# A gated product (GLU): groups of four rows in three 64 KiB slots in place of two-row tiles with slots of their own for the output

## The chip, the cores and the metric

The kernel runs on one core of a Trainium2 chip. The metric is the device time of one execution in microseconds (us). The three runs of the kernel before took 933.14, 933.66 and 934.35 us; their median is 933.66 us. A profile of one more execution says where the time goes.

## What is computed

```python
def setup_inputs():
    return {
        "x": np.random.randn(8192, 8192).astype(np.float32),
    }

def reference(x: np.ndarray) -> np.ndarray:
    a, b = np.split(x, 2, axis=-1)
    return a * (1 / (1 + np.exp(-b)))
```

Each row of x has 8192 numbers; the left 4096 are multiplied by the sigmoid of the right 4096. 268.4 MB are read and 134.2 MB are written, in fp32. Nothing is used twice.

## The kernel before

Everything is in `_tiles`. A tile is 256 rows: two consecutive rows on each of the 128 partitions (R = 2, line 27), so one load brings 64 KiB to each partition, 8 MiB in all, and one store takes 32 KiB from each, 4 MiB in all. There are 32 tiles. On chip there are two input slots `x_sb` of 64 KiB per partition and two output slots `o_sb` of 32 KiB per partition (lines 34 and 35), 192 KiB together; tile i uses slots i % 2.

Per tile there are four kinds of work:

- the load (line 53), a DMA issued by SyncE (SP). It waits until the product of tile i - 2 has read the slot;
- the sigmoid (line 71) on ScalarE (ACT), in place on the right half of each row;
- the product (line 72) on VectorE (DVE), out of the input slot into the output slot;
- the store (line 65), a DMA issued by ACT, after the product.

Inner tiles do both rows at once, one instruction of 8192 elements per partition on each engine. The first and the last tile are cut into four parts of 2048 elements, and in the last tile each part is stored by itself (lines 60 to 63 and 84 to 86). One small copy of 16 x 512 bytes from x to out (line 41) goes through ACT's DMA queue ahead of all else; its bytes are overwritten later.

The order on each engine is the order of the code. `implied` (line 37) drops waits that follow from others; lines 75 to 79 put the wait for a free output slot on the sigmoid in odd tiles. SP's DMAs form one queue and ACT's another; both run on the same 16 DMA engines. A DMA of 128 partitions is 128 packets, eight on each engine, and one more packet per engine that raises the semaphore. `_launch_early` moves the first load to the start of the program and `_close_on_sync` shortens its end; neither is touched.

Of the kernel before, what the change touches and what calls it, by code (L numbers as in the profile page):

```python
# [8 lines left out]
def _tiles(ctx, tc, x, out):  # L9

    nc = tc.nc
    P = nc.NUM_PARTITIONS  # L20
    DEP = mybir.DependencyInfo(mybir.DependencyClass.Sync, mybir.DependencyReason.DATA)
    fp32 = mybir.dt.float32
    SIG = mybir.ActivationFunctionType.Sigmoid

    n_rows, n_cols = x.shape
    half = n_cols // 2
    R = 2
    SLOTS = 2
    n_tiles = n_rows // (P * R)
    x_t = x.rearrange("(n p r) m -> n p (r m)", p=P, r=R)  # L30
    out_t = out.rearrange("(n p r) m -> n p (r m)", p=P, r=R)

    pool = ctx.enter_context(tc.tile_pool(name="io", bufs=1))
    xs = [pool.tile([P, R * n_cols], fp32, name=f"x_sb{k}") for k in range(SLOTS)]
    os = [pool.tile([P, R * half], fp32, name=f"o_sb{k}") for k in range(SLOTS)]

    def implied(later, *earlier):
        for e in earlier:
            tc.declare_no_dep(later.ins, e.ins, reason="follows from the waits that are kept")

    warm = nc.scalar.dma_start(out=out[0:16, 0:P], in_=x[0:16, 0:P])
    tc.keep_in_program_order(warm)

    gone = [{k: [] for k in ("loads", "sigs", "muls", "stores")} for _ in range(SLOTS)]
    last_stores = [[] for _ in range(SLOTS)]
    for i in range(n_tiles):
        old = gone[i % SLOTS]
        freed = last_stores[i % SLOTS]
        now = {k: [] for k in old}
        rows = xs[i % SLOTS].rearrange("p (r h m) -> p r h m", r=R, h=2)  # L50
        packed = os[i % SLOTS].rearrange("p (r m) -> p r m", r=R)

        load = nc.sync.dma_start(out=xs[i % SLOTS], in_=x_t[i])
        implied(load, *old["loads"], *old["sigs"])
        now["loads"].append(load)

        if 0 < i < n_tiles - 1:
            parts = [(slice(0, R), slice(0, half))]
        else:
            w = half // 2  # L60
            parts = [
                (slice(r, r + 1), slice(c * w, (c + 1) * w)) for r in range(R) for c in range(2)
            ]
        def store(cols):
            ins = nc.scalar.dma_start(out=out_t[i, :, cols], in_=os[i % SLOTS][:, cols])  # L65
            now["stores"].append(ins)

        chunks = []
        for k, (r, c) in enumerate(parts):
            b = rows[:, r, 1, c]  # L70
            sig = nc.scalar.activation(out=b, in_=b, func=SIG)  # L71
            mul = nc.vector.tensor_mul(out=packed[:, r, c], in0=rows[:, r, 0, c], in1=b)  # L72
            implied(sig, *old["sigs"], *old["muls"], *old["loads"])
            implied(mul, *old["muls"], *old["loads"], *now["loads"])
            by_sigmoid = i % 2 == 1 and len(parts) == 1
            implied(mul, *(s for s in old["stores"] if by_sigmoid or s not in freed))
            if by_sigmoid:
                for s in freed:
                    tc.add_manual_dep(sig.ins, s.ins.name, DEP, reason="frees the output slot")
            tc.keep_in_program_order(sig)  # L80
            now["sigs"].append(sig)
            now["muls"].append(mul)
            chunks.append(slice(r.start * half + c.start, r.start * half + c.stop))
            if i == n_tiles - 1 and k > 0:
                store(chunks[k - 1])
        store(chunks[-1] if i == n_tiles - 1 else slice(0, R * half))
        for s in now["stores"]:
            implied(s, *old["loads"], *old["sigs"], *old["muls"], *now["loads"], *now["sigs"])
        for k in old:
            old[k] += now[k]  # L90
        last_stores[i % SLOTS] = now["stores"]


def _launch_early(nc):
# [68 lines left out]
@with_exitstack  # L163
def kernel(
    ctx: ExitStack,
    tc: tile.TileContext,
    x: bass.AP,
    out: bass.AP,
):
    nc = tc.nc  # L170
    with ExitStack() as pools:
        _tiles(pools, tc, x, out)
    tc.close()
    tc.compile()
    _launch_early(nc)
    _close_on_sync(nc)
# [30 lines left out]
```

## Time and profile before

| what | value | from |
|---|---|---|
| median of three runs | 933.66 us | the times |
| span of the profiled execution | 932.3 us | the page |
| first load lands, first sigmoid | 21.91 us | the timeline |
| issue of a store | 0.36 us of ACT's queue | the timeline |
| issue of a load to its landing | 42.2 us, median | the page's DMA issues |
| issue of a 4 MiB store to its landing | 34.8 us, median | the page's DMA issues |
| last load lands, last sigmoids | 915.17 us | the timeline |

The span runs from the first to the last instruction that the profiler saw, so it is a little shorter than the time of an execution. A load's time to landing includes what lies ahead of it in its queue and what the other queue moves at the same time: it isn't the time of 8 MiB alone. The page counts DMA in two ways, as the share of time in which the 16 engines hold a packet, and as GB/s. The records put all bytes of a packet at its start, so the GB/s of a stretch mean something only where the stretch is long or begins and ends between the starts of packets.

### The profile page before, as it was taken

The numbers are of one execution on the slowest core, as the hardware profiler recorded it, in microseconds if no ns is written. First come the engines' busy times: TensorE is split into PE (matmuls) and PEld (weight loads), VectorE is DVE, ScalarE is ACT, GpSimd is POOL, SyncE is SP. The second block draws the span as 40 slices with busy tenths as digits, with TensorE's granted clock in tenths as the row PEclk, the third lists the DMA queues.
The fourth block names the chain that finished last, engine by engine and source line by source line (L and its number), as shares of the span: only waits on it lengthen the run. The fifth ranks groups of instructions, "written<-read, shape, count | busy, mean of one in ns | idle before, by whom it ended". The sixth has DMA issues, their size and how long they took to land.

```text
span 932.3 us, 250 instructions
## 1 busy us (share of the span) xinstructions
DVE 278.6 (30%) x38; ACT 227.0 (24%) x39; POOL 0.2 (0%) x4
## 2 busy tenths in 40 slices
DVE  0333213333133331233312333123331233312333
ACT  1323330233311333113331133311333203332033
POOL 0000000000000000000000000000000000000000
DMA  9999999999999999999999999999999999999999
GB/s 405 427 450 427 418 457 408 450 427 427 450 418 437 427 427 450 427 427 453 444 408 430 441 456 428 416 458 408 450 427 427 450 416 439 427 433 444 426 429 405
DMA packets 9681, 402.67 MB, mean 432 GB/s; under 512 B 1088, under 2 KB 1104, under 8 KB 1104
## 3 DMA queue, kind: packets, MB, share of 16 engines
q1 hardware_dynamic: 4608, 268.44, 66.6%
q10 hardware_dynamic: 5072, 134.23, 33.4%
q14 instruction: 1, 0.01, 0.0%
HBM read 268.44 MB, written 134.23 MB: 432 GB/s over the span
## 4 chain that ended last, share of the span: by engine, by line
DMA 73%; DVE 15%; ACT 12%; issue 0%; ACTq 0%
DMA x_sb<-in_x_dram 73%; DVE o_sb L72 15%; ACT x_sb L71 12%; ACTq L65 0%; ACTq L71 0%
## 5 line engine op out<-in xcount | busy, mean ns | idle before, releaser
L72 DVE TENSOR_TENSOR o_sb<-x_sb 128x8192 f32<-128x8192 f32 (+1 forms) x38 | 278.6, 7344 | 647.6 <-ACT x_sb L71 647.6
L71 ACT ACTIVATE x_sb<-x_sb 128x8192 f32<-128x8192 f32 (+1 forms) x38 | 225.7, 5950 | 695.5 <-DMA x_sb<-in_x_dram 694.3
L71 ACT ACT_TABLE_LOAD x1 | 1.3, 1283 | 1.4 <-PEq L191 1.4
L191 POOL MEMSET const-bfloat16-1.0<- 128x1 bf16 x1 | 0.1, 102 | 0.0
L191 POOL MEMSET const-uint8-127<- 128x1 uint8 x1 | 0.1, 102 | 0.0
L191 POOL MEMSET const-float32-0.0<- 128x1 f32 x1 | 0.1, 99 | 0.2 <-issue 0.2
L191 POOL MEMSET const-float32-1.0<- 128x1 f32 x1 | 0.1, 99 | 0.0
## 6 DMA issues: line engine op xcount, KB each, us to landing
out_dram<-o_sb ACTq DMA_DIRECT2D x31, 4096.0 KB, 34.8
out_dram<-o_sb ACTq DMA_DIRECT2D x4, 1024.0 KB, 5.7
x_sb<-in_x_dram SPq DMA_DIRECT2D x32, 42.2
out_dram<-in_x_dram ACTq DMA_DIRECT2D x1, 8.0 KB, 9.0
```

The source lines that it names most:

```text
L71: sig = nc.scalar.activation(out=b, in_=b, func=SIG)
L72: mul = nc.vector.tensor_mul(out=packed[:, r, c], in0=rows[:, r, 0, c], in1=b)
L191: nc = _bacc.Bacc("TRN2", target_bir_lowering=False, num_devices=1)
```

## The change

A group is now 512 rows, four consecutive rows on each partition (R = 4), in 16 groups. It is loaded in two halves of two rows, each again 64 KiB per partition. There are three slots of 64 KiB: first halves go to slots 0 and 2 in turn, every second half to slot 1. The products of both halves are written into the first half's slot: its first row's product over that row's left half, and so on, until the slot holds the four output rows packed, 64 KiB per partition, which one store takes out. There are no output slots.

The first half is computed in two parts of 4096 elements, the second in four of 1024, 1024, 2048 and 4096. A second half's load waits for the products of the second half before it (slot 1 is read); a first half's load waits for the store of the group two before (slot 0 or 2). In the last group the first half's products are stored by themselves, and the second half is computed and stored in four parts of 2048. The number of loads stays 32; stores go from 31 of 4 MiB and four of 1 MiB to 15 of 8 MiB, one of 4 MiB and four of 1 MiB. ACT and DVE each go from 38 instructions to 96.

The core of the diff; dropped waits and lists are left out:

```diff
-    R = 2
-    SLOTS = 2
-    n_tiles = n_rows // (P * R)
+    R = 4
+    n_groups = n_rows // (P * R)
...
+    WIDE = 2 * n_cols
...
-    xs = [pool.tile([P, R * n_cols], fp32, name=f"x_sb{k}") for k in range(SLOTS)]
-    os = [pool.tile([P, R * half], fp32, name=f"o_sb{k}") for k in range(SLOTS)]
+    slots = [pool.tile([P, WIDE], fp32, name=f"slot{k}") for k in range(3)]
...
+    FIRST = [(0, 0, half), (1, 0, half)]
+    QUICK = [(0, 0, half // 4), (0, half // 4, half // 2), (0, half // 2, half), (1, 0, half)]
+    EVEN = [(r, c * half // 2, (c + 1) * half // 2) for r in range(2) for c in range(2)]
+
+    def load(g, h):
+        k = 1 if h else 2 * (g % 2)
+        old = gone[k]
+        ins = nc.sync.dma_start(out=slots[k], in_=x_t[g, :, h * WIDE : (h + 1) * WIDE])
+        implied(ins, *old["loads"], *old["sigs"])
+        if h == 0:
+            implied(ins, *old["muls"])
...
+    def compute(g, h, parts, after=None):
+        home, k = 2 * (g % 2), 1 if h else 2 * (g % 2)
...
+        for r, lo, hi in parts:
+            a = slots[k][:, r * n_cols + lo : r * n_cols + hi]
+            b = slots[k][:, r * n_cols + half + lo : r * n_cols + half + hi]
+            to = (2 * h + r) * half
             sig = nc.scalar.activation(out=b, in_=b, func=SIG)
...
+            mul = nc.vector.tensor_mul(out=slots[home][:, to + lo : to + hi], in0=a, in1=b)
...
+            if after:
+                after(r, lo, hi)
...
+    def store(g, lo, hi, keep):
+        k = 2 * (g % 2)
+        ins = nc.scalar.dma_start(out=out_t[g, :, lo:hi], in_=slots[k][:, lo:hi])
...
+    load(0, 0)
+    for g in range(n_groups):
+        last = g == n_groups - 1
+        if g == 0:
+            load(0, 1)
+        compute(g, 0, FIRST)
+        if last:
+            store(g, 0, 2 * half, True)
+        if g == 0:
+            load(1, 0)
+        held = []
+
+        def piece(r, lo, hi):
+            if held:
+                store(g, *held.pop(), True)
+            held.append(((2 + r) * half + lo, (2 + r) * half + hi))
+
+        compute(g, 1, EVEN if last else QUICK, piece if last else None)
+        if last:
+            store(g, *held.pop(), True)
+            break
+        free[2 * (g % 2)] = []
+        store(g, 0, R * half, True)
+        load(g + 1, 1)
+        if g + 2 < n_groups:
+            load(g + 2, 0)
```

More of the change, by code (lines that the diff above doesn't have):

```diff
@@ L20, in _tiles @@
     P = nc.NUM_PARTITIONS
-    DEP = mybir.DependencyInfo(mybir.DependencyClass.Sync, mybir.DependencyReason.DATA)
     fp32 = mybir.dt.float32
@@ L26, in _tiles @@
     half = n_cols // 2
-    R = 2
-    SLOTS = 2
-    n_tiles = n_rows // (P * R)
+    R = 4
+    n_groups = n_rows // (P * R)
     x_t = x.rearrange("(n p r) m -> n p (r m)", p=P, r=R)
     out_t = out.rearrange("(n p r) m -> n p (r m)", p=P, r=R)
+    WIDE = 2 * n_cols
     pool = ctx.enter_context(tc.tile_pool(name="io", bufs=1))
-    xs = [pool.tile([P, R * n_cols], fp32, name=f"x_sb{k}") for k in range(SLOTS)]
-    os = [pool.tile([P, R * half], fp32, name=f"o_sb{k}") for k in range(SLOTS)]
+    slots = [pool.tile([P, WIDE], fp32, name=f"slot{k}") for k in range(3)]
+    gone = [{"loads": [], "sigs": [], "muls": [], "stores": []} for _ in slots]
+    free = [[] for _ in slots]
     def implied(later, *earlier):
@@ L42, in _tiles @@
     tc.keep_in_program_order(warm)
[L44 to L79, printed above, removed]
-            tc.keep_in_program_order(sig)
[L81 to L91, printed above, removed]
@@ new lines, in _tiles @@
+    FIRST = [(0, 0, half), (1, 0, half)]
[8 more added lines that the diff above has]
+            implied(ins, *old["muls"])
+        implied(ins, *(s for s in old["stores"] if s not in free[k]))
+        old["loads"].append(ins)
+        return ins
@@ new lines, in compute @@
+    def compute(g, h, parts, after=None):
+        home, k = 2 * (g % 2), 1 if h else 2 * (g % 2)
+        old, place = gone[k], gone[home]
+        now = old["loads"][-1]
+        done = []
+        for r, lo, hi in parts:
+            a = slots[k][:, r * n_cols + lo : r * n_cols + hi]
+            b = slots[k][:, r * n_cols + half + lo : r * n_cols + half + hi]
+            to = (2 * h + r) * half
+            sig = nc.scalar.activation(out=b, in_=b, func=SIG)
+            implied(sig, *old["sigs"], *old["muls"], *old["stores"], *old["loads"][:-1])
+            mul = nc.vector.tensor_mul(out=slots[home][:, to + lo : to + hi], in0=a, in1=b)
+            implied(mul, *place["stores"], *place["loads"], *old["loads"])
+            implied(mul, *place["sigs"])
+            tc.keep_in_program_order(sig)
+            tc.keep_in_program_order(mul)
+            tc.add_manual_dep(mul.ins, sig.ins.name, DEP, reason="the product reads it")
+            old["sigs"].append(sig)
+            for m in {id(old): old, id(place): place}.values():
+                m["muls"].append(mul)
+            done.append(mul)
+            if after:
+                after(r, lo, hi)
+        return done
@@ new lines, in store @@
+    def store(g, lo, hi, keep):
+        k = 2 * (g % 2)
+        ins = nc.scalar.dma_start(out=out_t[g, :, lo:hi], in_=slots[k][:, lo:hi])
+        implied(ins, *gone[k]["loads"], *gone[k]["sigs"])
+        tc.keep_in_program_order(ins)
+        gone[k]["stores"].append(ins)
+        if keep:
+            free[k].append(ins)
+    DEP = mybir.DependencyInfo(mybir.DependencyClass.Sync, mybir.DependencyReason.DATA)
+    load(0, 0)
[22 more added lines that the diff above has]
+            load(g + 2, 0)
```

## The prediction

> **What bounds the kernel now.** I read the page first, then the groups by shape, the chain of waits and the stretches by time.
>
> ```profile
> span 932.3 us, 250 instructions
> ...
> DVE 278.6 (30%) x38; ACT 227.0 (24%) x39; POOL 0.2 (0%) x4
> ...
> DMA  9999999999999999999999999999999999999999
> ...
> q1 hardware_dynamic: 4608, 268.44, 66.6%
> q10 hardware_dynamic: 5072, 134.23, 33.4%
> ```
>
> Loads (q1, issued by SP) and stores (q10, issued by ACT) hold the 16 DMA engines for 66.6 + 33.4 = 100% of the span. The compute engines are at 30% and 24%. The chain of waits looks different at first:
>
> ```profile
> 60.70 42.21 DMA x_sb<-in_x_dram
> ...
> 102.99 7.04 ACT x_sb L71
> ...
> 110.05 8.70 DVE o_sb L72
> ...
> 118.77 42.10 DMA x_sb<-in_x_dram
> ```
>
> It puts sigmoid and product on the path, 58 us per two tiles. But a load takes 42 us to land only because the engines are shared; the stretches show what 58 us are made of (columns: length, busy DVE, ACT, POOL, clock, DMA share, GB/s):
>
> ```profile
> 28.20:33.00 4.80, 4.55 (x3) 1.02 (x1) 0.00 (x0) 1.00 1.01 437
> 33.00:39.00 6.00, 0.00 (x0) 0.00 (x0) 0.00 (x0) 1.00 0.99 350
> 39.00:45.00 6.00, 0.00 (x0) 0.08 (x1) 0.00 (x0) 1.00 1.01 437
> 60.70:118.70 58.00, 17.34 (x2) 14.06 (x2) 0.00 (x0) 1.00 1.00 434
> 118.70:176.70 58.00, 17.42 (x3) 14.06 (x2) 0.00 (x0) 1.00 1.00 434
> 176.70:785.80 609.10, 182.54 (x22) 147.61 (x21) 0.00 (x0) 1.00 1.00 434
> ```
>
> 434 GB/s over 609 us without a dip: the bound is the bytes, 402.67 MB, and a shorter compute chain saves nothing. One row matters later. Between 33 and 39 us only 350 GB/s moved, though the engines count as busy: 6.0 x (437 - 350) / 437 = 1.2 us are missing. That is just after the first store:
>
> ```profile
> 23.86 8.90 DVE L72 TENSOR_TENSOR o_sb<-x_sb 128x2048 f32<-128x2048 f32 x4 [23.86 <-ACT x_sb L71]
> 32.79 0.36 ACTq L65 DMA_DIRECT2D out_dram<-o_sb  x1
> ```
>
> The trace's packet records show it on one engine (start us, ns, queue, bytes):
>
> ```
> 30.839 2418 load  65536
> 33.253 2418 load  65536
> 35.667 3429 load  65536
> 39.093 1213 store 32768
> 40.302 2418 load  65536
> 42.716 1213 store 32768
> ```
>
> Load packets start every 2.414 us; a load and a store packet together take 3.624 us, so a store packet takes 1.210. The store issued at 32.79 comes in after two more load packets, and the one ahead of it is 1.01 us longer. All 16 engines show such a packet there, 0.97 to 1.2 us too long (mean about 1.07). No later store does: a store lands 34.8 us after its issue and the next is issued 29 us after it, so the store queue never runs empty again.
>
> **The change, part by part.** Let t0 be the landing of group g's second half.
>
> Bytes and packets. Loads stay 32 transfers of 128 packets of 64 KiB. Stores become 15 of 128 packets of 64 KiB, one of 32 KiB packets, four of 8 KiB packets; before 31 and four. Per engine 248 packets of 32 KiB become 120 of 64 KiB and 8 of 32 KiB. By spacing, two of 32 KiB cost 2 x 1210 - 2414 = 6 ns more than one of 64; by recorded length 2 x 1213 - 2418 = 8 ns. 120 x 6 to 8 ns = 0.6 to 1.0 us gained, plus 15 transfers fewer that each end in a 9 ns packet, 0.1 us. I take -0.7 us.
>
> The compute of a second half. Shapes not in the trace come from the two that are:
>
> ```profile
> L72 DVE TENSOR_TENSOR o_sb<-x_sb 128x8192 f32<-128x8192 f32 x30 | 260.8, 8692 | 608.5 <-ACT x_sb L71 608.5
> L71 ACT ACTIVATE x_sb<-x_sb 128x8192 f32<-128x8192 f32 x30 | 210.9, 7029 | 653.2 <-DMA x_sb<-in_x_dram 653.2
> L72 DVE TENSOR_TENSOR o_sb<-x_sb 128x2048 f32<-128x2048 f32 x8 | 17.9, 2287 | 39.1 <-ACT x_sb L71 39.1
> L71 ACT ACTIVATE x_sb<-x_sb 128x2048 f32<-128x2048 f32 x8 | 14.8, 1901 | 42.3 <-DMA x_sb<-in_x_dram 41.1 <-DVE o_sb L72 0.9 <-issue 0.3
> ```
>
> A straight line gives ACT 0.192 us + 0.835 ns per element, DVE 0.152 us + 1.042 ns. For 1024, 1024, 2048, 4096 elements: sigmoids end at 1.05, 2.10, 4.00, 7.61; products at 2.27, 3.49, 6.29 and 7.61 + 4.42 = 12.0. So store(g) and load(g+1,1) are issued at t0 + 12.1, where before 15.8 us passed. Nothing is gained or lost by that itself: the cover is load(g+1,0), the only transfer then running, 8 x 2.414 = 19.3 us. The slack is 7 us less the issue's own delay; without it each late us would stop all engines. A first half (two pairs of 4096, about 12.5 us) gates no transfer except in the last group. Total DVE work, about 288 us, stays under the DMA.
>
> The joining of the store queue. This is new. Store(g) is alone in its queue and done about 8 pairs of 64 KiB packets later, 8 x 4.83 = 39 us, while stores are 58 us apart: the queue is empty for some 19 us in every group. So every store enters an empty queue beside running loads, as only the first did before. Bounds for the price: 1.2 us (above), and 0, since the 512-byte copy of L41 also entered that queue, between two load packets of 2418 ns each, with no gap. I take 1.07, the first store's: same queue, same direction out of SBUF, same neighbour; the small copy goes from HBM to HBM. Before there was one, after there are 15: 14 x 1.07 = +15.0 us. It is lost outright, as the engines have no idle time to make it up.
>
> The load that waits for a store. Load(g+2,0) now waits in SP for store(g). Behind it in SP is only load(g+2,1), wanted a group later. As for store 0, two load packets go ahead after the issue at t0 + 12.1 (packets 5 and 6 of load(g+1,0)); then the store's eight alternate with packet 7 and six of load(g+1,1). Two are left when the store ends: 4.8 us, or 2.4 if it joins a packet later. Against it stand 0.5 us, by which the 16 engines end apart, and the way from issue to first packet: 1.0 us for the first load (idle engines) up to 2.9 us (store 0 must be known when the packet at 35.67 starts, 35.67 - 32.79). Worst case 0.5 + 2.9 - 2.4 = 1.0 us a group, 14 us; otherwise nothing. I take nothing. The Trainium skill, "DMA: Bandwidth & Descriptors", section "Latency and other measured facts", gives about 600 ns to the first byte on this path, which would leave this load in time in either case; the trace shows 1.0 us or more.
>
> Rows of the loads now lie 128 KiB apart instead of 64; those of the stores 64 instead of 32. The trace has both 32 and 64 KiB, at 1210 ns per 32 KiB and 2414 per 64, so no cost of pitch shows; I take 0, with a tenth of a per cent (0.9 us) as bound either way. The same section of the skill speaks against wide pitches: 207 GB/s at 512 KiB where 214 was full. By that 3.3% the 619 us of loads per engine (256 x 2.414) would grow by an estimated 20 us; at 128 KiB no run here shows it.
>
> Ends. The first load's start is untouched; three loads queue at once, 58 us of work, and the second lands at 21.9 + 19.3 = 41.2, so store 0 is issued at 41.2 + 12.1 = 53.3. At the other end the half store (9.7 us) covers the last four pieces: their products end 4.2, 6.5, 8.8 and 11.1 us after the last landing, as before, and some 6.9 + 9.7 us of stores are left by then. 0.
>
> **Sum.** 932.3 - 0.7 + 15.0 = 946.6 us of span. The runs' median is 1.4 us above the span (933.66 - 932.3): 948.0 us.
>
> **Rivals.** First, the 1.1 us are paid once, because they belong to the first use of the path out of SBUF. For it: the small copy entered without a gap. Against: that queue had been used already when the 1.1 us appeared, and steady alternation shows no cost, so a restart is what remains. Then only the packets count: 933.66 - 0.7 = 933.0, no change that can be told. It decides when a store's entry costs under (1.87 + 0.7) / 14 = 0.18 us. Second, load(g+2,0) pays too, entering a queue with at most two packets left: another 14 x 1.07, or up to 14 us by arriving late, 948.0 + 15 = 963. Against: 30 loads of before were issued into a queue with some four packets left (a load lands 13 us after the next's issue) and cost nothing. Third, the loads' pitch: 5 us or more on top; no row speaks for it.
>
> **How the numbers follow.** Forecast 0.42; paid once 0.37; load late or joining 0.17; pitch 0.04. A measurement of this kernel tells 0.2%, 1.87 us, from no change. Paid once gives "same" 0.33 and, if both gains are at their upper bound and more, "faster" 0.04; all else is slower, 0.63. The forecast alone would be 944 to 950 (0.8 to 1.2 us a store). The range reaches to the paid-once case at 932.3 and over the load's at 965, leaving out about a tenth.
>
> **What would show it.** Right: once per group, some 3 to 7 us after the store's issue, a 6 us stretch near 350 GB/s beside 437, groups about 59.1 us apart, and 434 GB/s between. Paid once: groups 58.0 us apart. Load late: stretches with a DMA share well under 1 after a store's landing. Wrong altogether: a product chain so long that load(g+1,0) has landed before store(g) is issued.

## The result and the profile after

The changed kernel takes 962.88 us (median of five runs, 960.78 to 968.62) against 933.66 us: 1.032 times as long, 95% interval 1.0303 to 1.0337. The forecast was 948.0 us; the time lies in the range given, near its upper end, and the loss of 29.2 us is twice the forecast 14.3. The runs also spread over 8 us where those of before spread over 1.2.

The page of after, the lines that answer to those of before:

```profile
span 960.8 us, 327 instructions
...
DVE 286.8 (30%) x96; ACT 232.4 (24%) x97; POOL 0.2 (0%) x4
...
q1 hardware_dynamic: 4608, 268.44, 67.2%
q10 hardware_dynamic: 2912, 134.23, 32.3%
```

The bytes are the same and the engines hold packets for 99.5% of a span that is 28.5 us longer. So most of the loss isn't idle time in this count: packets take longer. The chain of waits has the same form as before, with load waits near 48 us:

```profile
232.47 47.62 DMA slot<-in_x_dram
...
280.11 7.32 ACT slot L62 x4
...
291.90 48.82 DMA slot<-in_x_dram
```

The stretches from one store's issue to the next (length first, DMA share and GB/s last) show where it starts:

```profile
52.89:112.07 59.18, 17.93 (x6) 14.43 (x6) 0.00 (x0) 1.00 1.00 425
112.07:170.61 58.54, 17.93 (x6) 14.43 (x6) 0.00 (x0) 1.00 1.00 427
170.61:232.47 61.86, 17.93 (x6) 14.43 (x6) 0.00 (x0) 1.00 0.99 417
232.47:291.91 59.44, 17.93 (x6) 14.43 (x6) 0.00 (x0) 1.00 0.99 413
291.91:352.55 60.64, 17.93 (x6) 14.43 (x6) 0.00 (x0) 1.00 0.99 419
```

58.0 us is what a group's bytes need at 434 GB/s. The first stretch holds the first store and loses 1.2; the second is nearly clean; from the third on each loses 1.3 to 3.9.

The packet records allow a closer account. "Lost" is here, in us per engine and as a mean over the 16, what packets took beyond the usual 2.418 us (1.213 for 32 KiB) and the gaps between packets. The whole run lost 1.95 + 0.25 us before, and 26.3 + 4.3 after. In after, by place (the load is the first half's, issued when its slot's store has landed; each window is the 8 us from the issue):

```
store at      load before it at   lost at the load   lost at the store
 52.9          (queued long ago)    -                 1.13
112.1           95.4               0.00               0.11
170.6          156.4               0.70               1.29
232.5          215.8               0.46               1.63
291.9          276.7               1.14               1.13
...
893.4          877.7               0.76               0.99
sum of all 15                     11.4               17.3
```

The second row is the telling one. That store entered an empty queue like all others and cost 0.1 us. What sets the other thirteen apart is that the load ahead of each came late. Their stores cost 1.2 us on average.

### The profile page after: what moved, and what is told of

Same layout as the page of the kernel before. It is cut to its first block, busy times and chain, and to the rows that moved or that the text cites. A ratio compares the mean times of both kernels' runs of the same rounds, so it can differ in the third digit from the quotient of the medians.

```text
span 960.8 us, 327 instructions
## 1 busy us (share of the span) xinstructions
DVE 286.8 (30%) x96; ACT 232.4 (24%) x97; POOL 0.2 (0%) x4
## 4 chain that ended last, share of the span: by engine, by line
DMA 75%; ACT 11%; DVE 8%; another core or an unknown queue 5%; issue 0%; ACTq 0%; DVEq 0%; SPq 0%
DMA slot<-in_x_dram 66%; ACT slot L62 11%; DMA out_dram<-slot 9%; DVE slot L64 8%; ACTq L80 0%; DVEq L64 0%; SPq L45 0%
## 5 line engine op out<-in xcount | busy, mean ns | idle before, releaser
L64 DVE TENSOR_TENSOR slot<-slot 128x2048 f32<-128x2048 f32 (+2 forms) x96 | 286.8, 3002 | 668.1 <-ACT slot L62 666.4
L62 ACT ACTIVATE slot<-slot 128x2048 f32<-128x2048 f32 (+2 forms) x96 | 231.1, 2468 | 718.7 <-DMA slot<-in_x_dram 717.4
## 6 DMA issues: line engine op xcount, KB each, us to landing
out_dram<-slot ACTq DMA_DIRECT2D x15, 44.3
```

Of the source, the lines that this page charges most:

```text
L64: mul = nc.vector.tensor_mul(out=slots[home][:, to + lo : to + hi], in0=a, in1=b)
```

## The experiments

Three theories at the start. A: a store's entry into an empty queue costs about 1.15 us, as predicted. B: the turn from loads to a store costs, whatever the queue. C: the 64 KiB store packets, the wider rows or the products in place cost.

**One queue** (e1). The 15 large stores go by SP, into the loads' queue:

```diff
-        ins = nc.scalar.dma_start(out=out_t[g, :, lo:hi], in_=slots[k][:, lo:hi])
+        queue = nc.scalar if g == n_groups - 1 else nc.sync
+        ins = queue.dma_start(out=out_t[g, :, lo:hi], in_=slots[k][:, lo:hi])
```

> Theory A: a DMA that enters an empty queue while the other queue runs holds up every engine by about 1.15 us (17.3 us over 15 stores in the trace of after), and the uneven hold-ups make the next first half's load late (11 us). With the 15 large stores issued by SP into the loads' own queue, which never runs empty, both are gone; one entry is left (the last group's stores on ACT's queue), as in before. 933.66 - 0.7 for the longer packets = 933.0 us, within 1 us. Theory B: the price is for turning from loads to a store, whatever the queue; it stays, and only the late loads go: 963 - 11 = 952. Theory C: the 64 KiB store packets, the rows 128 KiB apart or the products written in place cost: about 963, as after.

942.81 us, ratio 1.0098 (1.0083 to 1.0113): 20 us less than after. The first store still lost 1.05 us, though its queue was full; the later ones 0.28 at most, and several nothing. So B falls, and C as the main cause, since packets, rows and places are those of after. Of the 9.8 us above A's figure 7.8 are gaps between packets, most of them at the end, 265 GB/s in the last of 40 slices:

```profile
GB/s 416 432 429 418 446 438 410 446 438 429 426 438 435 429 429 440 438 416 446 429 438 426 438 438 421 438 443 432 424 440 438 435 421 446 435 435 424 438 426 265
```

**Row loads** (e2). Before, each load cut into two DMAs of one row:

```diff
-        load = nc.sync.dma_start(out=xs[i % SLOTS], in_=x_t[i])
-        implied(load, *old["loads"], *old["sigs"])
-        now["loads"].append(load)
+        for r in range(R):
+            cols = slice(r * n_cols, (r + 1) * n_cols)
+            load = nc.sync.dma_start(out=xs[i % SLOTS][:, cols], in_=x_t[i, :, cols])
+            implied(load, *old["loads"], *old["sigs"])
+            now["loads"].append(load)
```

> Before, with each load cut into two DMAs of one row, so that its packets are 32 KiB like the store's. The engines take packets from the two queues in turn, so a store now gets half instead of a third of the bytes and is done in about 20 of 29 us: the store queue runs empty in every tile. Theory A and theory B: 30 more entries x 1.15 = 34.5, plus 256 more packets per engine x 5 ns = 1.3: 933.66 + 36 = 970 us, some us more if loads come late. Theory C (nothing here is 64 KiB apart from before's, nothing in place): 933.66 + 1.3 = 935.

959.01 us, ratio 1.0267 (1.0232 to 1.0302). With nothing of the change in it but packets of one size in both queues, before loses 25 us. Not 36: the records show that only every second store found its queue empty, and from the one at 127.1 us on each of these lost 0.7 to 2.4 us, idle time counted; the stores between lost 0.2 at most. The load ahead ended some 3 us after those stores' issue, so that both queues ran out at about the same time: this run can't tell an empty store queue from an empty load queue as the cause.

**Half stores** (e3). After, each half stored once it is computed, in 32 KiB packets:

```diff
-        if last:
-            store(g, 0, 2 * half, True)
+        if not last:
+            free[2 * (g % 2)] = []
+        store(g, 0, 2 * half, True)
...
-        free[2 * (g % 2)] = []
-        store(g, 0, R * half, True)
+        store(g, 2 * half, R * half, True)
```

> After, with each half of a group stored as soon as it is computed: 30 stores with 32 KiB packets, one per 29 us, which a load's 64 KiB packets leave a third of the bytes, so that the store queue stays full as in before. Theories A and B: the 16 us of entries go; the first half's load still waits for a store, but engines stay together: 933.66 to 940. Theory C: rows 128 KiB apart and products in place are still there, store packets are 32 KiB: about 963 if the former two cost, 934 if it was the store packets (e1 tells these apart).

934.19 us, ratio 1.0005 (0.9996 to 1.0014): the whole loss is gone, with groups of four, three slots, products in place and the pieces kept. The same long stretch, first in e3, then in after:

```profile
176.70:785.80 609.10, 188.13 (x62) 151.43 (x62) 0.00 (x0) 1.00 1.00 434
```

```profile
176.70:785.80 609.10, 179.28 (x60) 144.31 (x60) 0.00 (x0) 1.00 1.00 418
```

The DMA share reads 1.00 in both. Only GB/s tells them apart.

**Tiny copies** (e4). e1 with a 16 x 512-byte copy, HBM to HBM, on ACT's empty queue in each of 15 groups:

```diff
+        if not last:
+            tiny = nc.scalar.dma_start(out=out[n_rows - 16 : n_rows, 0:P], in_=x[0:16, 0:P])
+            tc.keep_in_program_order(tiny)
```

> The kernel with one queue, and in each of 15 groups one small copy (16 x 512 bytes, HBM to HBM) on ACT's otherwise empty queue, between the halves. If any entry into an empty queue costs 1.15 us per engine: 15 x 1.15 = +17 us over the kernel with one queue. If only an entry of large packets out of SBUF costs: +0.1 us.

943.38 us, ratio 1.0104 (1.0089 to 1.0119), beside 1.0098 for e1: no difference that can be told.

**One queue, end mended** (e5). e1, with the last second half's load ahead of the last large store:

```diff
+        if g == n_groups - 2:
+            load(g + 1, 1)
         store(g, 0, R * half, True)
-        load(g + 1, 1)
+        if g < n_groups - 2:
+            load(g + 1, 1)
```

> The kernel with one queue left the DMA engines idle for 7.8 us, most of it in its last slice (265 GB/s), where the last second half's load stands behind the last large store in the same queue and lands with little left to move beside its compute. With these two exchanged in the queue, the large store covers that compute: 942.8 - 7.5 = 935.3 us, within 1.5. If the idle time is not from this order: 942 to 943.

936.23 us, ratio 1.003 (1.0018 to 1.0041); gaps fell from 7.8 us to 0.15. So the end was what e1 had left.

**A row by ACT** (e6). e5, with the fourth row of products by ACT's queue:

```diff
-        store(g, 0, R * half, True)
+        store(g, 0, 3 * half, True)
+        store(g, 3 * half, R * half, True)
...
-        queue = nc.scalar if g == n_groups - 1 else nc.sync
+        queue = nc.scalar if g == n_groups - 1 or lo == 3 * half else nc.sync
```

> The one above, but the fourth row of each group's products (a quarter of the store, 16 KiB packets out of SBUF) goes by ACT's queue, which is empty at that time; no load is late here. Theory A (each entry of a store into an empty queue costs 1.15 us): 15 x 1.15 = +17 us over e5_one_queue_end. Theory D (an entry is cheap, 0.1 us as in the second group of after, unless the engines have been driven apart by a late load): +1 to +4 us, of which 1.2 is for packets of 16 and 48 KiB.

937.44 us, ratio 1.0045 (1.003 to 1.0061): 1.2 us over e5 where A asked for 17. Fifteen stores out of SBUF, of 16 KiB packets, entered an empty queue beside running loads, and nearly nothing was lost. A falls; for packets of 64 KiB the groups of e8 below show the same. Theory D of this expectation remains: an entry is dear only where a late load has driven the engines apart.

**Dry loads** (e7). e5, with the first half's load held until the load ahead of it has landed, so that its queue runs dry:

```diff
-            load(g + 1, 1)
+            ahead = load(g + 1, 1)
         if g + 2 < n_groups:
-            load(g + 2, 0)
+            late = load(g + 2, 0)
+            tc.add_manual_dep(late.ins, ahead.ins.name, DEP, reason="runs the queue dry")
```

> e5_one_queue_end, but each first half's load from the third on is issued only when the second half's load ahead of it has landed, so that the one queue runs dry once in 14 groups; no store enters an empty queue beside running loads. Price of a dry queue from the first load of all: 1.0 us from issue to first packet, 0.7 us that the first packet is longer, 0.5 us by which engines end apart: 14 x 2.2 = +31 us over e5_one_queue_end; at the 0.9 us a group that the trace of after shows: +12 us.

987.5 us, ratio 1.0575 (1.056 to 1.0589): 51.3 us over e5, or 3.66 in each of 14 groups, far above the 2.2 expected. The packets of one engine show why (gap: idle before the packet, us):

```
start us   ns    queue bytes   gap
 97.083   2418   SP    65536
 99.497      9   SP        4
101.526   2924   SP    65536   2.02    the late load
104.446   2422   SP    65536
...
116.555   2420   SP    65536
118.971   3769   SP    65536           the packet ahead of the next store
122.743   2418   SP    65536
```

The stretches of all 16 engines, cut between packets, say the same:

```profile
96.55:104.20 7.65, 2.36 (x2) 3.75 (x4) 0.00 (x0) 1.00 0.74 274
104.20:116.30 12.10, 6.72 (x2) 3.56 (x2) 0.00 (x0) 1.00 1.00 433
116.30:122.25 5.95, 0.00 (x0) 0.00 (x0) 0.00 (x0) 1.00 0.99 352
122.25:136.75 14.50, 8.85 (x2) 7.12 (x2) 0.00 (x0) 1.00 1.00 434
```

Two packets of 2.414 us fit into the first stretch and two into the third: 7.65 - 4.83 = 2.8 us are lost at the dry queue (2.0 idle, 0.8 on the first packet), and 5.95 - 4.83 = 1.1 at the store that follows, 15 us later. In between and after, all runs at full rate. The second loss has the DMA share of a full engine. Here the store entered no empty queue: it stood in the loads' own. This is theory E: once engines have run dry, the next store costs again. Here all 16 engines ran dry each time, and the 16 parts of each of these loads landed within 1.0 us of one another, so that engines driven apart, theory D, aren't needed for it.

**Eight pieces** (e8). After, the second half in eight pieces of 1024, so that the store is issued 10.3 us after the landing instead of 11.8:

```diff
-    QUICK = [(0, 0, half // 4), (0, half // 4, half // 2), (0, half // 2, half), (1, 0, half)]
+    QUICK = [(r, c * half // 4, (c + 1) * half // 4) for r in range(2) for c in range(4)]
```

> After, with the second half computed in eight pieces of 1024, so that the store is issued about 9.6 us after the landing instead of 11.8: one load packet (2.4 us) earlier, so that one more packet is left to cover the load that waits for the store. Theory A: the late loads' 11 us go, the 17 us of entries stay: 952. Theory D (entries are dear only because late loads drove the engines apart): both go, 933 to 938. If the load is late for another reason than this margin: 963.

946.0 us (943.62 to 952.34), ratio 1.0144 (1.0111 to 1.0177), between the theories, because some loads still came late: none up to 460 us and four in a row after that. Within this one run the two kinds of group stand side by side, all with 64 KiB packets in an empty queue:

```
store at   lost at the load before it   lost at the store
110.5      0.00                         0.00
285.3      0.00                         0.04
460.6      0.00                         0.06
519.4      0.43                         1.06
578.6      0.68                         1.16
638.0      0.31                         1.71
697.8      0.42                         1.07
756.9      0.00                         0.03
```

Of the 14 stores after the first, nine followed a load that lost under 0.1 us: eight of them lost 0.08 or less, one 0.26. The five others, behind loads that lost 0.1 to 0.7, lost 0.7 to 1.7. Two stretches without a late load and two with one:

```profile
110.52:168.50 57.98, 18.02 (x10) 14.80 (x10) 0.00 (x0) 1.00 1.00 434
...
285.30:343.27 57.97, 18.02 (x10) 14.80 (x10) 0.00 (x0) 1.00 1.00 434
...
578.65:637.95 59.30, 18.02 (x10) 14.81 (x10) 0.00 (x0) 1.00 1.00 423
637.95:697.78 59.83, 18.02 (x10) 14.80 (x10) 0.00 (x0) 1.00 1.00 417
```

How far the engines are apart, theory D, doesn't decide it. The 16 parts of the load before the store at 460.6 landed over 2.5 us, and that store lost 0.06; in after, those before the store at 170.6 landed over 1.2 us, and it lost 1.29; in e3 they landed over 2.5 to 3.2 us for every load but the first, and its stores after the first lost nothing.

Nor does theory E hold engine by engine. In after, the load issued at 215.78 found four engines without a packet; at the store that followed, the packet ahead of it was 1.2 to 2.0 us too long on all sixteen. In e8 the load issued at 503.52 found one, and the store at 519.4 cost all sixteen 0.7 to 1.3. What is shown is an order of events in the whole kernel: a load that comes late to an emptied queue, then a dear store. Why the one brings the other stays open.

**Second halves by rows** (e10). After, only the second half's load cut into two DMAs of one row, for more cover:

```diff
+        cut = 1 if h == 0 else 2
+        for c in range(cut):
+            lo, hi = c * WIDE // cut, (c + 1) * WIDE // cut
+            ins = nc.sync.dma_start(out=slots[k][:, lo:hi], in_=x_t[g, :, h * WIDE + lo : h * WIDE + hi])
```

> After, with only the second half's load cut into two DMAs of one row (32 KiB packets). A store of 64 KiB packets then passes it two to one and is done some 10 us earlier, so that four load packets are left to cover the load that waits for it; the store still enters an empty queue in each of 15 groups. Theory E: the price is for engines that have run dry, as in the kernel with dry loads (there a dry queue cost 2.0 us idle, 0.7 us on the first packet, and 1.1 us on the first store packet after it, 3.8 together); without dry engines an entry is nearly free. 933.66 - 0.7 + 128 more packets x 5 ns = 933.6, at most 936. Theory A (an entry costs 1.15 us in itself): 933.6 + 16 = 950.

956.89 us, ratio 1.0256 (1.0242 to 1.027): a miss. No load came late (0.04 us at most), and the second and third store lost 0.00 and 0.03, as E says. But from the fourth on they lost 0.1 to 0.8, store packets later in the groups were drawn out too, and the end stood idle for 7.3 us as in e1. The engines had drifted apart: the 16 parts of one load landed within 0.6 us at the start and over 13 us at 367 us. So there is a loss without a dry queue, which theory E leaves out; that the drift causes it is argued from their coming together, and no run here settles it.

**A warm store** (e9). Before, its first small copy taken out of SBUF:

```diff
-    warm = nc.scalar.dma_start(out=out[0:16, 0:P], in_=x[0:16, 0:P])
+    seed = pool.tile([16, P], fp32, name="seed")
+    nc.vector.memset(seed, 0.0)
+    warm = nc.scalar.dma_start(out=out[0:16, 0:P], in_=seed)
```

> Before, with the small first copy taken out of SBUF (16 x 512 bytes of zeros) instead of out of x, in the first microseconds, when the engines are still starting. If the 1.1 us at the first store are paid by the first turn to SBUF, however small: paid where engines start anyway, 933.66 - 1.1 = 932.6. If it takes a large store, or belongs to the first load packets: 933.7, no change.

933.62 us, ratio 1.0003 (0.9994 to 1.0012), and the first store still lost 1.03 us. A tiny turn to SBUF early in the run doesn't pay it in advance.

No version beat before: e3 ties with it.

## Why the prediction missed

**What bounds the kernel** held: bytes over the DMA engines, compute hidden.

**Bytes and packets** held in kind: 64 KiB store packets take 2.418 us as loads do. The 0.7 us is too small to be seen by itself.

**The compute of a second half** held: 12.0 us worked out, 11.8 measured (landing at 41.09, store at 52.89).

**The joining of the store queue** was right in amount and wrong in cause; that the amount fits is luck. The step said 15 x 1.07 = 16 us for stores that enter an empty queue; the records have 17.3. (The mean over the sixteen packets of before is 1.10 rather than 1.07, which adds 0.4 us to the sum.) But an entry is nearly free (e6, e8, the second group of after, the tiny copies). The first store pays even where its queue is full (1.05 us in e1); that it pays for the start of the engines from nothing is the reading that e7 suggests. I had one event with two candidate reasons, the first store and the empty queue, and "no later store does" spoke for both alike.

**The load that waits for a store** is the step that failed: "I take nothing". The loads came late in 13 groups and lost 11.4 us, and each was followed by a dear store. Two things were wrong in it. First the cover. Where the engines were together it was as worked out: store 0 landed by 95.4, the load ahead until 99.9, so 4.5 us were left (4.8 predicted) and nothing was lost. But the forecast let the engines end 0.5 us apart. One group on, fifteen engines took the store's first packet 4.1 to 4.9 us after its issue and one took it a whole packet later, at 7.0. The store then landed over 3.6 us, its last part at 156.0, and 2 us of the load ahead were left:

```profile
156.43 76.37 SPq L45 DMA_DIRECT2D slot<-in_x_dram  x4
158.81 7.31 ACT L62 ACTIVATE slot<-slot 128x1024 f32<-128x1024 f32 x4 [27.11 <-DMA slot<-in_x_dram]
...
170.61 0.36 ACTq L80 DMA_DIRECT2D out_dram<-slot  x1
```

In the first line the late load is issued; in the second the load ahead of it has landed, 2.4 us later, and some engines have nothing. The prediction saw that a join could fall a packet later (2.4 us of cover) but not that engines would differ by it. Second the price. "Worst case 1.0 us a group, 14 us" counted idle time alone. The late loads lost 11.4 us, inside that bound (3.8 of it idle, the rest longer first packets), and the thirteen stores behind them 16.1 more, which the forecast had booked under the entry into an empty queue. Together 27.5, and 0.1 for the second store, against the 28.5 us by which the span grew.

**The rivals.** The second (the load pays too, 963 us) has the right time and half of the mechanism; it got 0.17. The first (the 1.1 us are paid once) was right that an entry isn't what costs, and would have been right on the time if the loads had kept up, as e3 does at 934.2. The pitch isn't it: e3 has loads with rows 128 KiB apart, e5 has the stores of after too, and both are within 3 us of before.

**The ends** held: 0.2 us of gaps at the end of after.

## What to carry to other kernels

Here two DMA queues shared the engines packet by packet, and so divided the bytes by packet size. With twice as many bytes read as written, packets of 64 and 32 KiB kept both queues full to the end (before and e3). Making the smaller ones as large as the others, to have fewer of them, drained the store queue early: a store landed 44.3 us after its issue (median), and the next came about 60 us after it. The load that waited for the store's end then lacked cover, other transfers to keep the engines busy. Count cover for the slowest engine, with a whole packet of spread and not with the spread of a quiet trace. And where the DMA share reads 1.00, look at GB/s beside it: a drawn-out packet counts as busy.

## What the runs showed of the hardware

In e7 engines that ran dry lost 2.0 us idle and 0.8 on their first packet, and then 1.1 us again at the next store, 15 us and six packets of nearly full rate later, in the same queue, 14 times. In after and e8 the second loss fell on all 16 engines where only a few had run dry. The start of each program looks like the same event: 0.4 to 0.8 us on the first load packets and 1.0 to 1.3 ahead of the first store, in all versions but e6, where it was 0.5. Why the second payment exists isn't settled. It isn't the entry into an empty queue (0.08 us or less at eight of e8's stores of 64 KiB packets), and a tiny store beforehand doesn't take its place (e9: 1.03 us).
